# A two-block fp32 network on one core: the scheduler's cost estimates are replaced on three engines

## The chip, the core and the metric

The kernel runs on one core of a Trainium2 chip. A core has five engines that run side by side, each working through its own list of instructions in order: TensorE (PE in the profile; PEld is its loading of weights), VectorE (DVE), ScalarE (ACT), GpSimd (POOL) and SyncE (SP), which here issues the DMAs. Engines wait for each other through semaphores. The metric is the device time of one execution in microseconds (us); smaller is better.

## The reference, cut to what matters

Two blocks on 256 tokens of width 1024, all in fp32. The first block has a mixer (a short convolution, stick-breaking attention and retention, merged by gates), attention to a memory of 256 rows, and a squared-ReLU MLP of width 4096. The second block has a state-space mixer (SSD, 8 groups), a feed-forward net with a causal convolution (width 2816), a latent attention of 8 heads, and a second such feed-forward net; each is followed by a layer norm.

```python
h = rmsnorm(x, norm_mix_g); proj = h @ w_in            # 10 x 512 + 3 x 1024 columns
x = x + sum(sigmoid(gates) * up(conv, stick, ret)) @ w_o
x = x + memory_attention(rmsnorm(x), rmsnorm(mem), w_q, w_kv, w_out)
x = rmsnorm(x + square(relu(rmsnorm(x) @ w_up)) @ w_down)
h = layer_norm(ALPHA * x + ssd_mixer(x));  h = layer_norm(ALPHA * h + conv_ffn(h))
h = layer_norm(ALPHA * h + mla_attention(h)); h = layer_norm(ALPHA * h + conv_ffn(h))
```

## The kernel before, in words

**Weights.** All weight matrices lie in one array, cut into chunks of at most 128 partitions x 2048 floats (1 MB) in the order of their use. A chunk is loaded by a DMA into a raw tile (`wr`, two buffers) and split in two halves: ScalarE casts a half to the high part (`wh`, method `copy`), VectorE subtracts it from the raw half to get the low part (`wl`, method `sub`). Four split chunks are held at most (`HELD`). A product is three matmuls on TensorE (`mm3`): high x high, high x low, low x high. Activations are split the same way (`ah`, `al` and others), after transposes on TensorE into the `sm` banks of PSUM; the products go to the `mm` banks.

**Order of the work.** The program is written out at build time by a planner; on the chip every engine runs its list as it was written. The main line of the program walks through the matmuls stage by stage. After each group of matmuls it calls `tick`, which may insert, behind what has been issued so far, steps of background tasks (evacuations of PSUM, convolutions, softmax, norms, each a Python generator that yields where it would have to wait) and splits of weight halves. A step whose inputs come from TensorE, ScalarE or VectorE is inserted when the planner believes that they will be ready.

**What the planner believes.** `Plan` keeps one clock per engine (`t`). `enter` is called for each instruction: it starts at the later of the engine's clock and of the time when its operands are there (`after`, with a handover from engine to engine out of the table `LATE`, 0.05 to 0.22 us) and moves the clock by `cost`. `cost` has one formula for each engine. A matmul of 256 or more columns costs its columns at 2400 per us. On ScalarE an instruction costs its elements at 1200 per us and 0.05 us (from PSUM) or 0.093 us, and 0.093 us more for each further operand and for a sum. On VectorE it is elements at 960 per us and 0.068 us, and 0.06 us for each operand that is a column.

**Where the clocks are used.** `can_step` lets a task step if its inputs are ready by the clock of TensorE or of its own engine, and its engine is not over `AHEAD` (1.0 us) in front of TensorE; tasks marked `first` (norms) may be taken a little early (`EARLY`). `split_next` inserts a cast or a subtraction. It calls one late by a deadline: `need` is now plus the matmul time of the chunks that are split (`sums`, in units of `UNIT`) less the matmul time done (`work`), and 0.95 us are counted for a cast and 1.15 us for a subtraction. A split that is not late must leave room in front of a `first` task and must not be over `FILL` (0.8 us) ahead. At the end of a stage, the last chunks are kept and used for both halves of the tokens (`TAIL`), so that the norm of the first half runs beside the second half's matmuls; `skew` accounts for them.

The profile puts nearly every instruction on L284, the line of the helper that records them, so its groups are told apart by tiles.

Of the kernel before, what the change touches and what calls it, by code (L numbers as in the profile page):

```python
# [8 lines left out]
BF16 = mybir.dt.bfloat16  # L9
# [15 lines left out]
LATE = {("pe", "act"): 0.2, ("pe", "dve"): 0.2, ("act", "pe"): 0.22, ("dve", "pe"): 0.15, ("pool", "dve"): 0.06,  # L25
        ("pool", "act"): 0.06, ("pool", "pe"): 0.05, ("act", "pool"): 0.18, ("dve", "pool"): 0.16, ("act", "act"): 0.15,
        ("pe", "pe"): 0.0, ("dma", "act"): 0.95, ("dma", "dve"): 0.95, ("dma", "pe"): 0.95, ("dma", "pool"): 0.95}
UNIT = 6 / 2400
AHEAD = 1.0
FILL = 0.8  # L30
SOON = 0.0
# [258 lines left out]
class Plan:  # L290
# [62 lines left out]
    def cost(self, kind, name, out, ins, args, kw):  # L353
        n = 1
        for s, c in out.ap[1:]:
            n *= c
        psum = any(x.space == PSUM for x in ins)
        aps = sum(1 for x in ins[1:] if x.free_size() == 1)
        if kind == "pe":
            if name == "transpose":  # L360
                return 0.11
            if kw["rhs"].dtype == F32:
                m = kw["lhsT"].shape[-1]
                return 4 * max(n, m) / 2400 * (0.53 if m <= 64 else 1.0)
            return (n if n >= 256 or kw["rhs"].dtype == BF16 else 4 * n) / 2400
        if kind == "act":
            t = n / 1200 + (0.05 if psum else 0.093)
            if name in ("activation", "mul"):
                t += 0.093 * (len(ins) - 1) + (0.093 if "accum_out" in kw else 0)
            return t  # L370
        if kind == "dve":
            for x in ins[:1]:
                m = 1
                for s, c in x.ap[1:]:
                    m *= c
                n = max(n, m)
            if name == "reciprocal":
                return n / 160 + 0.07
            fast = name in ("tensor_copy", "tensor_scalar", "tensor_scalar_mul", "tensor_scalar_add") and not psum
            return n / (1920 if fast else 960) + 0.068 + (0.06 * aps if "scalar" in name else 0)  # L380
        if kind == "pool":
            return (0.3 + 0.16 * n if n < 3 else 0.6) if name == "tensor_tensor" else n / (280 if name == "tensor_copy" else 960) + 0.11
        return 0.0
# [88 lines left out]
class Kern:  # L472
    def __init__(self, nc, tc, a, dbg=None):
# [11 lines left out]
        self.work = self.skew = 0.0  # L485
        self.sums = np.concatenate([[0.0], np.cumsum([len(ks) * max(n, P) * UNIT for _, ks, _, n, _ in self.plan])])

# [197 lines left out]
    def mm3(self, outs, lhs, rhs, first, last, weights=True):  # L685
        passes = ((0, 0), (0, 1), (1, 0))
        if weights:
            self.work += sum(o.free_size() for o in outs) * 3 / 2400
        for q, (i, j) in enumerate(passes):
            for n, o in enumerate(outs):  # L690
                self.nc.tensor.matmul(o, lhsT=lhs[i], rhs=rhs[j][n] if isinstance(rhs[j], list) else rhs[j],
                                      start=first and q == 0, stop=last and q == 2, skip_group_check=True)
# [27 lines left out]
    def xstat(self, tag, nks, lhs, blocks, tail=0, after=None, before=None):  # L720
# [29 lines left out]
        if tail:  # L750
            chs = []
            for tau in range(2):
# [3 lines left out]
                for c in range(tail):  # L756
# [19 lines left out]
                    else:  # L776
                        self.skew = 0.0 if c == tail - 1 else self.skew + nk * chs[c][0].shape[2] * UNIT / 2
                    self.tick()
        return ps

    def wmixed(self, tag, act, nk, consumers, tasks=None):
# [4 lines left out]
        for tau in range(2):  # L786
            for c in range(n):
# [8 lines left out]
                if tau == 0:  # L796
                    self.skew = 0.0 if c == n - 1 else self.skew + nk * wh.shape[2] * UNIT / 2
                if tau:
# [637 lines left out]
    def ssd(self, h, act):  # L1436
# [259 lines left out]
        for tau in range(2):  # L1696
            got = [0]
            for i, (half, c) in enumerate(last):
                ch = so(half, c, (tau,), chs[i] if tau else None)
                chs.append(ch)  # L1700
                if tau == 0:
                    self.skew = 0.0 if i == 2 else self.skew + 2048 * UNIT / 2
                if i:
# [80 lines left out]
    def attention(self, h, act):  # L1784
# [106 lines left out]
        for tau in range(2):  # L1891
            for tag, nk, src, blocks in (("qr", 3, cq, [(0, 512)]), ("v", 2, ckv, [(0, 512), (512, D)])):
# [12 lines left out]
                else:  # L1905
                    self.skew = nk * wh.shape[2] * UNIT / 2 if tag == "qr" else 0.0
                if tag == "qr":
# [180 lines left out]
```

## Time and profile before

| | |
|---|---|
| median of 3 runs | 1233.27 us (1233.09 to 1234.08) |
| the profiled execution's own time | 1233.43 us |
| its span in the profile | 1231.7 us |
| TensorE busy | 1214.2 us, 99% of the span |
| weight loads busy | 1109.8 us, 90% |
| VectorE busy | 852.7 us, 69% |
| ScalarE busy | 718.0 us, 58% |
| DMA queue of the weights and inputs | 51.1% of 16 engines' time |

The profiled execution is one execution beside the timed ones. Its span runs from the first to the last instruction, and 1.73 us of its own time lie outside the span. Busy time is the union of the instructions' own intervals; where instructions of one engine overlap in the records, a mean duration is longer than the distance from one start to the next.

### The profile page before, as it was taken

The numbers are of one execution on the slowest core, as the hardware profiler recorded it, in microseconds if no ns is written. First come the engines' busy times: TensorE is split into PE (matmuls) and PEld (weight loads), VectorE is DVE, ScalarE is ACT, GpSimd is POOL, SyncE is SP. The second block draws the span as 40 slices with busy tenths as digits, with TensorE's granted clock in tenths as the row PEclk, the third lists the DMA queues.
The fourth block names the chain that finished last, engine by engine and source line by source line (L and its number), as shares of the span: only waits on it lengthen the run. The fifth ranks groups of instructions, "written<-read, shape, count | busy, mean of one in ns | idle before, by whom it ended". The sixth has DMA issues, their size and how long they took to land.

```text
span 1231.7 us, 20769 instructions
## 1 busy us (share of the span) xinstructions
PE 1214.2 (99%) x8468; PEld 1109.8 (90%) x8468; DVE 852.7 (69%) x1378; ACT 718.0 (58%) x1181; POOL 53.2 (4%) x85
## 2 busy tenths in 40 slices
PE   7999999999999999999999999999999999999997
PEld 5979999989989998888999898999988888999986
DVE  5666848677747765446887797888855866888853
ACT  5666546446536554345789765666643665666631
POOL 0011000000000000000111201000000000000000
PEclk9999999999999999999999999999999999999999
DMA  7643355546444556524556545555673442455560
GB/s 257 246 159 132 142 198 221 185 163 227 172 154 167 211 193 226 183 105 172 224 206 237 190 172 197 180 185 193 216 262 105 164 184 106 171 206 190 209 251 34
DMA packets 35425, 227.71 MB, mean 185 GB/s; under 512 B 4321, under 2 KB 4993, under 8 KB 11522
## 3 DMA queue, kind: packets, MB, share of 16 engines
q1 hardware_dynamic: 35330, 226.39, 51.1%
q8 instruction: 66, 1.08, 0.3%
q14 instruction: 29, 0.24, 0.1%
HBM read 225.27 MB, written 1.10 MB: 184 GB/s over the span
## 4 chain that ended last, share of the span: by engine, by line
PE 93%; DVE 3%; DMA 1%; ACT 1%; issue 0%; POOL 0%; SPq 0%; POOLq 0%; DVEq 0%; ACTq 0%
PE mm L284 84%; PE sm L284 9%; DMA wr<-wts 1%; DVE wl L284 1%; DVE x L284 1%; DVE tk L284 0%; POOL rs L284 0%; ACT wh L284 0%; SPq L284 0%; DVE dtw L284 0%; DVE ln L284 0%; DVE al L284 0%; ACT L284 0%; ACT tk L284 0%; POOLq L2084 0%
## 5 line engine op out<-in xcount | busy, mean ns | idle before, releaser
L284 DVE TENSOR_TENSOR wl<-wr,wh 128x1024 fp32r<-128x1024 f32 (+3 forms) x408 | 478.7, 1196 | 174.2 <-ACT wh L284 173.5
L284 ACT CAST wh<-wr 128x1024 fp32r<-128x1024 f32 (+3 forms) x408 | 403.9, 1030 | 160.4 <-PE mm L284 88.6
L284 PE MATMUL mm<-ah,wh 128*128 128x256 f32 (+1 forms) x1496 | 417.1, 279 | 0.0
L284 PE MATMUL mm<-ah,wl 128*128 128x256 f32 (+1 forms) x1496 | 413.6, 276 | 0.1
L284 PE MATMUL mm<-al,wh 128*128 128x256 f32 (+1 forms) x1496 | 413.4, 276 | 0.0
L284 PEld LDWEIGHTS mm<-ah,wh 128*128 128x128 f32 (+1 forms) x1496 | 280.2, 187 | 1.6 <-issue 1.1
L284 PEld LDWEIGHTS mm<-al,wh 128*128 128x128 f32 (+1 forms) x1496 | 280.3, 187 | 0.4
L284 PEld LDWEIGHTS mm<-ah,wl 128*128 128x128 f32 (+1 forms) x1496 | 280.2, 187 | 0.4 <-DVE wl L284 0.3
L284 DVE SCALAR_TENSOR_TENSOR r<-mm,pcol,r 128x255 f32<-128x255 f32 (+2 forms) x212 | 86.9, 474 | 35.1 <-ACT r L284 35.1
L284 PE MATMUL mm<-wl,ah 128*128 128x512 f32 (+3 forms) x320 | 106.1, 338 | 3.0 <-DVE wl L284 2.9
L284 PE MATMUL mm<-wh,ah 128*128 128x512 f32 (+3 forms) x320 | 108.7, 346 | 0.0
L284 PE MATMUL mm<-wh,al 128*128 128x512 f32 (+3 forms) x320 | 106.3, 338 | 0.5 <-DVE al L284 0.5
L284 PE MATMUL mm<-wh,gTh 128*128 128x512 f32 x304 | 96.2, 391 | 0.0
L284 PE MATMUL mm<-wl,gTh 128*128 128x512 f32 x304 | 95.6, 389 | 0.0
L284 PE MATMUL mm<-wh,gTl 128*128 128x512 f32 x304 | 95.5, 389 | 0.0
L284 ACT ACTIVATE r<-mm,pcol 128x256 f32<-128x256 f32 x96 | 48.9, 560 | 43.3 <-PE mm L284 43.3
L284 PEld LDWEIGHTS mm<-wl,ah 128*128 128x128 f32 x320 | 60.4, 190 | 10.0 <-DVE wl L284 4.6
L284 PEld LDWEIGHTS mm<-wh,gTl 128*128 128x128 f32 x304 | 57.1, 188 | 11.9
L284 PEld LDWEIGHTS mm<-wl,gTh 128*128 128x128 f32 x304 | 57.1, 188 | 11.8
L284 PEld LDWEIGHTS mm<-wh,gTh 128*128 128x128 f32 x304 | 56.7, 188 | 12.0 <-issue 0.6
L284 PEld LDWEIGHTS mm<-wh,al 128*128 128x128 f32 x320 | 60.2, 189 | 7.0 <-DVE al L284 1.2
L284 PEld LDWEIGHTS mm<-wh,ah 128*128 128x128 f32 x320 | 60.3, 189 | 6.5 <-issue 0.7
(296 smaller groups left out, 1576.6 us busy)
## 6 DMA issues: line engine op xcount, KB each, us to landing
wr<-wts SPq DMA_DIRECT2D x186, 1024.0 KB, 4.8
wr<-wts SPq DMA_DIRECT2D x11, 768.0 KB, 4.3
gb<-prow SPq DMA_DIRECT2D x12, 512.0 KB, 6.5
dec<-rows SPq DMA_DIRECT2D x8, 768.0 KB, 8.1
wr<-wts SPq DMA_DIRECT2D x4, 704.0 KB, 4.1
wr<-wts SPq DMA_DIRECT2D x4, 512.0 KB, 6.5
tk<-mem SPq DMA_DIRECT2D x2, 512.0 KB, 7.3
out<-x SPq DMA_DIRECT2D x4, 256.0 KB, 2.1
```

The lines of the kernel that those rows point to most:

```text
L284: r = f(*args, **kw)
```

## The change

The planner's estimates are changed. A matmul of 256 or more columns costs 17/16 of what it cost, and so do the unit of the deadline (`UNIT`) and the matmul time done (`work`). On ScalarE elements cost 1/1110 us in place of 1/1200, and the fixed part is 0.1 us for every source. On VectorE the fixed part is 0.11 us in place of 0.068. All other numbers of the planner, and all instructions that the program holds, stay; only the order in which they are written can differ (and, through the ScalarE clock, where a table is loaded in advance).

```diff
-UNIT = 6 / 2400
+UNIT = 6 * 17 / 16 / 2400
...
-            return (n if n >= 256 or kw["rhs"].dtype == BF16 else 4 * n) / 2400
+            return (n * 17 / 16 if n >= 256 else n if kw["rhs"].dtype == BF16 else 4 * n) / 2400
         if kind == "act":
-            t = n / 1200 + (0.05 if psum else 0.093)
+            t = n / 1110 + 0.1
...
-            return n / (1920 if fast else 960) + 0.068 + (0.06 * aps if "scalar" in name else 0)
+            return n / (1920 if fast else 960) + 0.11 + (0.06 * aps if "scalar" in name else 0)
...
         if weights:
-            self.work += sum(o.free_size() for o in outs) * 3 / 2400
+            self.work += sum(o.free_size() for o in outs) * 3 * 17 / 16 / 2400
```

## Rows read from the trace of the kernel before

**Rows 1.** The page's first part: busy us (share of the span) xinstructions of each engine.

```profile
PE 1214.2 (99%) x8468; PEld 1109.8 (90%) x8468; DVE 852.7 (69%) x1378; ACT 718.0 (58%) x1181; POOL 53.2 (4%) x85
```

**Rows 2.** Windows: stretch, its length, busy us (xinstructions) per engine, clock, DMA.

```profile
0.00:20.00 20.00, 13.48 (x42) 8.61 (x43) 10.75 (x24) 10.39 (x17) 1.57 (x7) 1.00 0.83 288
300.00:395.00 95.00, 94.94 (x631) 86.52 (x630) 60.84 (x85) 51.00 (x82) 1.10 (x2) 1.00 0.47 171
395.00:550.00 155.00, 155.00 (x989) 140.20 (x988) 87.29 (x92) 72.60 (x89) 0.55 (x1) 1.00 0.52 188
550.00:566.00 16.00, 15.55 (x84) 12.72 (x83) 9.12 (x15) 5.67 (x11) 0.55 (x1) 1.00 0.35 133
566.00:580.00 14.00, 13.87 (x119) 13.27 (x117) 8.38 (x20) 10.64 (x17) 0.00 (x0) 1.00 0.42 152
745.00:763.00 18.00, 17.84 (x86) 14.53 (x85) 11.45 (x21) 9.71 (x17) 1.63 (x2) 1.00 0.67 245
937.00:964.00 27.00, 25.62 (x140) 22.09 (x139) 20.39 (x45) 13.89 (x30) 2.68 (x3) 1.00 0.39 134
964.00:1030.00 66.00, 65.91 (x403) 56.25 (x403) 45.19 (x108) 41.05 (x93) 0.70 (x1) 1.00 0.46 168
1030.00:1062.00 32.00, 31.27 (x228) 28.76 (x227) 24.65 (x40) 20.31 (x33) 1.87 (x2) 1.00 0.37 132
1223.00:1231.70 8.70, 0.71 (x4) 0.25 (x2) 4.11 (x11) 2.02 (x6) 0.93 (x1) 0.83 0.17 61
```

**Rows 3.** Timeline of TensorE: start us, us, instruction; 36 and 16 matmuls lie between starts.

```profile
400.02 0.28 PE L284 MATMUL mm<-ah,wl 128*128 128x256 f32 x1
...
404.10 0.28 PE L284 MATMUL mm<-ah,wl 128*128 128x256 f32 x1
...
500.45 0.62 PE L284 MATMUL mm<-wh,gTh 128*128 128x512 f32 x2
...
504.07 0.62 PE L284 MATMUL mm<-wh,gTl 128*128 128x512 f32 x2
```

**Rows 4.** Groups by form: xcount, busy us, mean ns of one, idle before and releasers.

```profile
L284 DVE TENSOR_TENSOR wl<-wr,wh 128x1024 fp32r<-128x1024 f32 x376 | 451.0, 1222 | 157.8 <-ACT wh L284 157.1
...
L284 ACT CAST wh<-wr 128x1024 fp32r<-128x1024 f32 x376 | 380.0, 1050 | 154.3 <-PE mm L284 86.3 <-DMA wr<-wts 63.7 <-issue 2.6
...
L284 PE MATMUL sm<-cst,tk 128*128 128x128 f32 x116 | 17.9, 283 | 2.4 <-DVE tk L284 2.2 <-ACT tk L284 0.2
```

**Rows 5.** Timelines of VectorE and of ScalarE, us 1045 to 1061 (runs of equal instructions merged).

```profile
1045.72 2.35 DVE L284 TENSOR_TENSOR wl<-wr,wh 128x1024 fp32r<-128x1024 f32 x2
1047.99 1.28 DVE L284 TENSOR_TENSOR al<-sm,ah 128x512 fp32r<-128x512 f32 x2
...
1057.58 1.64 DVE L284 SCALAR_TENSOR_TENSOR r<-sm,pcol,r 128x255 f32<-128x255 f32 x4
1059.14 2.35 DVE L284 TENSOR_TENSOR wl<-wr,wh 128x1024 fp32r<-128x1024 f32 x2
...
1057.49 2.01 ACT L284 CAST wh<-wr 128x1024 fp32r<-128x1024 f32 x2
1059.39 1.04 ACT L284 ACTIVATE r<-sm,pcol 128x256 f32<-128x256 f32 x2
1060.30 0.60 ACT L284 COPY tk<-mm 128x512 f32<-128x512 f32 x1
```

**Rows 6.** Chain that ended last, around us 949 and 1040: start us, us, what.

```profile
949.07 0.81 DVE wl L284
...
1040.02 1.14 DVE wl L284
```

**Rows 7.** TensorE's waits over the span: us in total, times, longest us.

```profile
PE sm L284 <- DVE x L284: 0.7, 3, 0.3
```

**Rows 8.** Timeline of TensorE, us 942 to 944: two matmul pairs, the first behind four transposes.

```profile
942.14 0.70 PE L284 MATMUL mm<-wh,gTh 128*128 128x512 f32 x2
...
943.15 0.62 PE L284 MATMUL mm<-wh,gTl 128*128 128x512 f32 x2
```

## The prediction

> **What bounds the kernel now.** I read the page's busy times first, then cut the span into windows at the joints between stages, then looked inside the windows at the single engines' timelines. The first view says that TensorE is busy for 1214.2 of 1231.7 us [rows 1]; 17.5 us are idle. The windows say where [rows 2]: 6.52 us in the first 20 us (the first weights and inputs are still arriving, with the DMA engines 83% busy), 7.99 us in the last 8.7 us (the last layer norm, behind the last matmul), and 0.06 + 0.45 + 0.13 + 0.16 + 1.38 + 0.09 + 0.73 = 3.00 us in seven windows between. All these windows are joints: a norm ends one stage and begins the next, and TensorE meets transposes or a low weight half that are not there yet. Everywhere else TensorE is fed without a gap; 395 to 550 us is such a stretch, 989 matmuls and no idle time.
>
> So the kernel is bound by the list of its matmuls. Nothing in the diff removes an instruction; it can only reorder the lists of the three engines. What it can win is idle time of TensorE at the joints, and a little where transposes are put between matmuls.
>
> A page of the Trainium skill speaks against reading it so: "Perfetto Trace Analysis", section "Identifying the Most-Contended Engine", calls matmul busy time a bad measure of what is left and takes the busy share of the weight loads instead. By that share, 90% [rows 1], an estimate of headroom would be 10% of the span, 122 us. The row of 395 to 550 us decides against it here: the loads are busy for 140.20 of 155.00 us [rows 2] while the 512-column matmuls inside it follow each other at their steady distance [rows 3]; the loads wait for matmuls, not the other way round.
>
> **What the change does to the estimates.** First the true numbers, as distances from start to start in full queues:
> - A 256-column matmul: 36 starts in 404.10 - 400.02 = 4.08 us, 113.3 ns; a 512-column one: 16 in 3.62 us, 226.3 ns [rows 3]. The old estimate is 256/2400 = 106.7 ns and 213.3 ns, 6% short; the new one 113.3 and 226.7 ns, right.
> - The subtraction of a weight half on VectorE: two in 1047.99 - 1045.72 = 2.27 us, 1.135 us each [rows 5]. Old 1024/960 + 0.068 = 1.135, right; new 1.177, 3.7% long.
> - A convolution step on VectorE (255 elements, PSUM, a column operand): four in 1.56 us, 0.390 [rows 5]. Old 0.394, right; new 0.436, 12% long.
> - The cast of a weight half on ScalarE: two in 1059.39 - 1057.49 = 1.90 us, 0.950 [rows 5]. Old 0.946, right; new 1024/1110 + 0.1 = 1.023, 7.6% long.
> - An activation of 256 elements from PSUM with scale and bias: two in 0.91 us, 0.455 [rows 5]. Old 0.213 + 0.05 + 0.186 = 0.449, right; new 0.517, 14% long.
>
> The durations of single instructions are longer: 1222 ns for the subtraction, 1050 ns for the cast [rows 4]. The new formulas move towards those. But consecutive instructions overlap by 0.09 to 0.10 us (1.222 - 1.135, 1.050 - 0.950), and the planner adds its costs one behind the other, while the handover to another engine stands in a table of its own that isn't touched. So on TensorE an estimate that was short becomes right, and on the other two, ones that were right become long.
>
> What decides an order is the ratio between engines. Before, VectorE and ScalarE looked 113.3/106.7 = 1.062 times as slow against TensorE as they are. After, VectorE looks 1.04 (subtractions, 451.0 of its 852.7 us [rows 1, 4]) to 1.12 times as slow, by shares about 0.53 x 1.037 + 0.47 x 1.10 = 1.07; ScalarE 1.076 (casts, 380.0 of 718.0 us) to 1.14, about 0.53 x 1.076 + 0.47 x 1.12 = 1.10. Taken together the change is very nearly one of the unit of time: all three clocks run 4 to 15% longer, and their ratios move by +1% and +3.5%. Only what keeps its size (handovers, the limits of 1.0 and 0.8 us, the 1.15 and 0.95 us of the deadline, transposes, DMA times) gets 6% smaller beside the rest. So I expect close decisions to tip here and there, with no drift.
>
> **The terms of the sum**, against the profiled execution's own 1233.43 us (0.16 us above the median of the runs):
> - The stretches with no idle time: 0. Cover: TensorE's own list of matmuls, full; a step that is moved there moves within the idle time of VectorE or ScalarE (67.7 and 82.4 us of 155.0 between 395 and 550 us [rows 2]).
> - Start and end: 0. The start waits for weights, the end is a chain with no weights left to order. From both sides: nothing to win without data; to lose, one subtraction in front of the second norm, 1.1 us [rows 5], which I take for unlikely.
> - The joints: from -3.00 us (all idle time closed [rows 2]) to +4.5 us (below). The deadline test: `need` grows by 1/16 of the split matmul time in stock (a 1 MB chunk is 48 matmuls of 113.3 ns, 5.4 us, so 0.3 us for each), against 0.04 or 0.08 us more for each split; splits count as late a little less often, so a subtraction may give way to a norm at 949 and 1040 us, where it now stands on the chain for 0.81 and 1.14 us [rows 6]. But behind the norm the same subtractions must still run before the next stage's matmuls, so most of that comes back. The waits of transposes for the norm, 0.7 us in all [rows 7], should shrink, as norm steps are now given more time. I take -0.5.
> - Insertions of transposes: the matmul pair behind four transposes takes 0.70 instead of 0.62 us [rows 8], so an insertion costs about 0.08 us beside its own work. One group alone has 116 transposes, 29 insertions by fours [rows 4]. If a dozen more or fewer stand alone, that is 1.0 us either way; I take 0.
> - Table loads and DMAs: the DMAs are issued in the same order from a subtraction's end; I take 0.
>
> Sum: 1233.43 - 0.5 = 1232.9; I say 1233.0.
>
> **The rivals.**
> - *The joints close.* With TensorE's own speed right, transposes and norm steps are put where their inputs are there, and the idle time goes: 1233.43 - 3.00 - 0.5 (a few insertions merged) = 1229.9. For it: the gaps are where short chains of 512-element steps meet TensorE. Against: the largest one, 1.38 us between 937 and 964 us, lies where VectorE is busy for 20.39 of 27.00 us [rows 2] with the few split buffers full; order alone hardly helps. 0.23.
> - *Subtractions land on the norms' chains* (the other sign). With ScalarE thought 7.6% slower at casts, a cast and its subtraction come one place later, and at the four joints with the thickest chains (windows at 550, 745, 937 and 1030 us) the subtraction falls between the steps of the norm, which TensorE waits for: 4 x 1.135 = 4.5 us, 1237.9. It decides from three joints of the four. For it: it happens already at two places [rows 6]. Against: the lateness test loosens. 0.21.
> - *TensorE's estimate is now too long*, so that the others seem fast and transposes are put in too early. If two thirds of the step of 6% were too much, 4%, a norm of up to 7.99 us, as at the end [rows 2], would come 0.3 us later than planned; if two in three of 29 insertions [rows 4] met that, it would be 5.8 us, 1239.2. The starts of 113.3 and 226.3 ns speak against it [rows 3]. The Trainium skill, "TensorE: Matmul & The Clock Gate", section "Back-to-back issue gap", would have it so: columns / 2.4 GHz + 2.5 ns, 109.2 and 215.8 ns. The trace does not agree: its excess is 6.6 and 13 ns and grows with the columns. 0.04.
> - *Nothing tips* or the tips cancel, which is also the case that the change doesn't do what it says, since it brings durations into a model that wants distances: 1233.4, part of the forecast.
>
> **How the numbers follow.** About 0.2% (2.5 us) is what a measurement of this kernel can tell from no change. The forecast (1233.0, own range 1231.0 to 1235.5) has 0.52, all of it within that bound; the joints that close 0.23, faster; the two slower rivals 0.25. So faster 0.23, same 0.52, slower 0.25. For 8 in 10 the range goes from 1229.6 (under the closed joints) to 1238.2 (just over the subtractions at all four).
>
> **What the profile after would show.** Right: TensorE with 2 to 4.5 us idle between 20 and 1223 us, the same count of instructions but perhaps a table load or two, starts 113 and 226 ns apart in the full stretches. The joint at 937 to 964 us keeps about 1 us. The first rival is right if the seven windows fall to under 0.6 us together; the second if a subtraction stands between two norm steps at three or four joints and the idle time there is over 5 us. I am wrong altogether if idle time appears inside a full stretch (the state-space stage has the busiest VectorE and ScalarE), where a tipped order would starve TensorE of split weights.

## The result and the profile after

The changed kernel takes 1259.32 us (median of 4 runs, 1258.19 to 1263.83) against 1233.32 us for the kernel before in the same comparison: ratio 1.0214 (95% interval 1.0202 to 1.0226), slower by 26 us. The forecast was 1233.0 us with a range from 1229.6 to 1238.2.

The page's first part, of the changed kernel (answers to [rows 1]; span 1256.8 us):

```profile
PE 1221.9 (97%) x8468; PEld 1113.5 (89%) x8468; DVE 854.0 (68%) x1378; ACT 719.1 (57%) x1178; POOL 49.6 (4%) x85
```

The lists hold the same work: 8468 matmuls, 1378 VectorE instructions, and three ScalarE instructions fewer (the planner loads a table in advance, by a dummy activation, four times instead of seven; the 24 table loads stay). The span grew by 25.1 us, of which TensorE's busy time is 1221.9 - 1214.2 = 7.7 us and its idle time 34.9 - 17.5 = 17.4 us. Both need a cause. The windows say where (columns as in [rows 2]: length, busy us of each engine, TensorE's granted clock, DMA share and GB/s):

```profile
0.00:20.00 20.00, 14.05 (x45) 8.91 (x46) 11.15 (x24) 10.44 (x18) 1.57 (x7) 1.00 0.83 294
370.00:398.00 28.00, 26.52 (x208) 25.07 (x207) 19.29 (x23) 16.12 (x24) 1.40 (x1) 1.00 0.41 151
398.00:550.00 152.00, 152.00 (x973) 137.56 (x972) 84.58 (x89) 71.84 (x88) 0.15 (x1) 1.00 0.54 192
550.00:572.00 22.00, 20.51 (x115) 17.00 (x114) 12.94 (x19) 9.05 (x16) 0.95 (x2) 1.00 0.40 145
572.00:675.00 103.00, 103.00 (x777) 94.81 (x776) 81.64 (x138) 89.63 (x172) 16.61 (x20) 1.00 0.59 215
675.00:690.00 15.00, 11.41 (x74) 10.07 (x73) 14.12 (x24) 13.00 (x21) 0.00 (x0) 0.89 0.57 198
762.00:798.00 36.00, 33.36 (x233) 30.32 (x232) 25.31 (x41) 19.82 (x34) 2.00 (x2) 1.00 0.40 152
955.00:990.00 35.00, 29.83 (x165) 25.91 (x164) 24.07 (x58) 15.81 (x35) 2.39 (x3) 1.00 0.39 135
1045.00:1080.00 35.00, 29.49 (x179) 26.84 (x179) 22.00 (x35) 16.52 (x28) 1.87 (x2) 0.90 0.42 151
1248.00:1256.80 8.80, 0.43 (x2) 0.01 (x1) 4.02 (x9) 1.92 (x6) 0.93 (x1) 0.72 0.16 61
```

Length less TensorE's busy time is its idle time: 5.95 us at the start and 8.37 at the end, nearly as before (6.52 and 7.99), and 1.48 + 1.49 + 3.59 + 2.64 + 5.17 + 5.51 = 19.88 us in six places between, where the kernel before has 3.00 us in all [rows 2]. Five are joints that it has too. One, at 675 to 690 us, ends the state-space stage, where the kernel before has no idle time. The long stretches between the joints (398 to 550, 572 to 675) stay full.

What TensorE waits for, in total over the span (us, times, longest):

```profile
PE mm L284 <- DVE wl L284: 11.8, 10, 3.2
PE sm L284 <- ACT r L284: 3.5, 1, 3.5
PE sm L284 <- ACT tk L284: 3.5, 3, 1.6
```

The first line is matmuls that wait for a weight half's low part; in the kernel before it is 2.9 us. The second is one wait, the new one at the end of the state-space stage. The third, 0.2 us before, is transposes that wait for a copy of their input on ScalarE. The norm, which the prediction watched, is not the main loser (transposes wait for its `x` for 0.6 us, against 0.7 [rows 7]); the weights are late.

**One joint followed (370 to 398 us).** Up to 372 us the two traces agree to some hundredths of a us. Then VectorE takes the residual additions `x` before the subtraction `wl`, which in the kernel before came first. Timelines of VectorE (dots stand for lines between), first the kernel before, then the changed one:

```profile
372.44 1.22 DVE L284 TENSOR_TENSOR wl<-wr,wh 128x1024 fp32r<-128x1024 f32 x1
...
374.77 1.22 DVE L284 TENSOR_TENSOR wl<-wr,wh 128x1024 fp32r<-128x1024 f32 x1
```

```profile
372.61 0.69 DVE L284 SCALAR_TENSOR_TENSOR x<-mm,x 128x512 f32<-128x512 f32 x1
...
375.77 1.22 DVE L284 TENSOR_TENSOR wl<-wr,wh 128x1024 fp32r<-128x1024 f32 x1
...
378.76 3.48 DVE L284 TENSOR_TENSOR wl<-wr,wh 128x1024 fp32r<-128x1024 f32 x3
```

The two halves of a chunk share one raw buffer, so the second half's subtraction (374.77 us before; changed, the first of the three at 378.76) is its last reader. There are two raw buffers (`RAW = 2`), and the DMA that refills one stands behind that subtraction. SyncE's queue, before and then changed:

```profile
376.01 14.42 SPq L284 DMA_DIRECT2D wr<-wts  x4
```

```profile
380.04 11.62 SPq L284 DMA_DIRECT2D wr<-wts  x4
```

The second half's subtraction starts 3.99 us later, the DMA 4.03. The chain that ended last, of the changed kernel, carries that on (start us, us, what):

```profile
380.04 4.78 DMA wr<-wts
...
384.90 1.05 ACT wh L284
...
385.98 2.37 DVE wl L284 x2
...
388.37 4.83 DMA wr<-wts
...
393.28 1.05 ACT wh L284
394.33 0.49 ACT t L284
394.82 0.94 ACT wh L284
395.76 0.53 ACT gTh L284
396.29 0.48 ACT tk L284
...
396.82 0.66 PE sm L284 x4
```

DMA, cast, subtraction, DMA, and then late casts stand between the steps of the next stage's gate, for which TensorE's transposes at 396.82 us wait. The first subtraction was moved by 3.3 us. Of the 1.48 us of idle time, 0.63 came at once (377 to 379 us, waits for the low part and for the norm), and 0.85 came 20 us later, at 396.82 us.

**The new stall (state-space stage).** The chain of the changed kernel at 678 to 687 us:

```profile
678.13 2.27 DVE wl L284 x2
...
680.66 0.80 DVE yTl L284 x2
...
681.49 1.98 ACT wh L284 x2
683.47 0.63 ACT yTh L284 x2
684.10 0.64 ACT r L284
...
684.78 1.99 PE sm L284 x8
```

Two casts (1.98 us) and two evacuations (0.63) stand ahead of the last gate activation on ScalarE, and TensorE waits 3.5 us. VectorE and ScalarE are busy for 14.12 and 13.00 of these 15 us, so little can be put off there without cost; that is an argument, as no run moves a step of this stretch alone.

**The busy time.** The granted clock explains most of the 7.7 us. Windows of 2 us behind the stall:

```profile
684.00:686.00 2.00, 1.22 (x6) 1.13 (x7) 2.00 (x3) 2.00 (x5) 0.00 (x0) 0.82 0.24 98
686.00:688.00 2.00, 2.00 (x7) 1.62 (x7) 2.00 (x4) 2.00 (x3) 0.00 (x0) 0.50 0.46 78
688.00:690.00 2.00, 2.00 (x11) 1.59 (x10) 2.00 (x3) 0.03 (x1) 0.00 (x0) 0.83 0.84 352
```

0.50 is 1.2 of 2.4 GHz. The three windows lack 0.18 + 0.50 + 0.17 = 0.85 of 2 us, up to 1.7 us of work. Of the 123 windows of 10 us from 20 to 1250 us, three are below 1.00: 680 to 690, 1060 to 1070 and 1070 to 1080 us, each at 0.83, together 3 x 1.7 = 5.1 us at most, since these windows count the clock of idle time too; the kernel before has none from 20 to 1220 us. The other 2.6 us are not resolved (0.57 of them is in the first 20 us; the transposes stand between the matmuls in 81 runs, against 82 before, so it is not more insertions).

### The profile page after: what moved, and what is told of

Read it like the earlier page. It is cut to its first block, busy times and chain, and to the rows that moved or that the text cites. A ratio compares the mean times of both kernels' runs of the same rounds, so it can differ in the third digit from the quotient of the medians.

```text
span 1256.8 us, 20781 instructions
## 1 busy us (share of the span) xinstructions
PE 1221.9 (97%) x8468; PEld 1113.5 (89%) x8468; DVE 854.0 (68%) x1378; ACT 719.1 (57%) x1178; POOL 49.6 (4%) x85
## 4 chain that ended last, share of the span: by engine, by line
PE 88%; DVE 5%; DMA 3%; ACT 2%; issue 1%; POOL 1%; SPq 0%; POOLq 0%; DVEq 0%; ACTq 0%
PE mm L284 79%; PE sm L284 9%; DMA wr<-wts 2%; DVE wl L284 2%; ACT wh L284 1%; DVE x L284 1%; POOL rs L284 1%; DVE r L284 0%; DVE tk L284 0%; ACT tk L284 0%; DVE al L284 0%; DMA cst<-cst 0%; ACT r L284 0%; ACT ah L284 0%; DVE ln L284 0%
## 5 line engine op out<-in xcount | busy, mean ns | idle before, releaser
L284 PEld LDWEIGHTS mm<-wh,gTh 128*128 128x128 f32 x304 | 56.7, 188 | 12.6 <-ACT r L284 0.9
L284 PEld LDWEIGHTS mm<-wh,gTl 128*128 128x128 f32 x304 | 57.1, 188 | 11.9
```

The costliest lines, as they stand in the source:

```text
L284: r = f(*args, **kw)
```

## The experiments

The letters in the expectations are theories. A: the planner's fixed limits, `FILL` = 0.8 us above all, keep their size while the clocks they are compared with run faster. B: the matmul estimate that was 6% short was a margin that kept weights early. C: the kernel before sits in a hollow, and a shift of either sign loses. D: an order flip is dear because a put-off subtraction holds its raw buffer and delays the next DMA. E, the prediction's own view: a flip costs at most a subtraction's length and is hidden. D': the deadline, which counts a chunk's casts and subtractions but not the DMA behind them, puts splits off too long. F: no order has room for both, the norm's steps and the splits.

**The parts alone.** `pe_only` takes the three TensorE terms of the diff, `dve_only` the one VectorE term, `no_dve` all but that; `fill_09` is the whole change with a wider limit. (In the tables, the ratio is to the kernel before in the same comparison, and the clock is TensorE's mean granted clock in the profiled execution.)

```
dve_only:  before,  + 0.068  ->  + 0.11
fill_09:   changed, FILL = 0.8  ->  FILL = 0.9
```

> Only TensorE's part of the change (matmul cost, unit of the deadline, work done times 17/16); ScalarE and VectorE keep the old estimates. Theory A (a subtraction at a joint misses the limit FILL of 0.8 us because VectorE's clock now stands further ahead; its raw buffer comes free later, the next weights land later, TensorE starves): 1229 to 1238 us. Rival B (the old, short matmul estimate was a hidden margin in the deadline; taking it away makes every split late): 1248 us or more.

> Only VectorE's part (0.11 in place of 0.068). Theory A: 1243 us or more, with idle TensorE at the joints. Rival B: 1230 to 1237 us, since TensorE's estimate is the old one.

> The whole change less VectorE's part. Theory A: 1243 us or less. Rival B: 1250 us or more, as TensorE's part is in it.

> The whole change, and the limit FILL at 0.9 us in place of 0.8, so that a subtraction is let in with VectorE's clock up to 0.9 us ahead. Theory A: 1245 us or less, and the joint at 370 to 398 us idle for less than 0.3 us (1.5 us with the change alone). Rival B: 1253 us or more, the limit is not what makes splits late.

| kernel | median us | ratio (95%) | clock |
|---|---|---|---|
| pe_only | 1245.98 | 1.0099 (1.0071 to 1.0128) | 0.998 |
| dve_only | 1256.10 | 1.0181 (1.0166 to 1.0196) | 0.991 |
| no_dve | 1249.37 | 1.0125 (1.0110 to 1.0141) | 0.995 |
| fill_09 | 1246.75 | 1.0104 (1.0087 to 1.0120) | 0.995 |

Every part loses, and the parts don't add: 12.2 us for TensorE's terms and 22.3 for VectorE's against 26.0 for all. VectorE's 42 ns nearly suffice alone, so most of the loss comes without B. But only `dve_only` came out as a theory said (A). `pe_only` (four runs from 1241.97 to 1250.52 us), `no_dve` and `fill_09` fell between A's and B's forecasts, and the 12.2 us for TensorE's terms fit neither. ScalarE's terms were not tried alone. Widening `FILL` by 0.1 us returns 12.6 us, and the joint at 370 us is full again:

```profile
370.00:398.00 28.00, 28.00 (x216) 26.66 (x214) 20.18 (x25) 16.97 (x25) 1.10 (x2) 1.00 0.43 151
675.00:690.00 15.00, 11.41 (x76) 10.38 (x75) 13.96 (x26) 13.96 (x23) 0.00 (x0) 0.80 0.50 175
```

The limit decides at that joint. It doesn't at 675 to 690 us, where 3.59 us idle stay.

**Small shifts, and all limits scaled.** Three kernels move one estimate of the kernel before; the fourth scales `AHEAD`, `FILL`, `EARLY` and the constants of the deadline and room tests of the changed kernel by 17/16, as the estimates were.

```
dve_plus4:        before, + 0.068  ->  + 0.072
dve_minus42:      before, + 0.068  ->  + 0.026
pe_half_percent:  before, the three TensorE terms * 201 / 200
```

> The kernel before with VectorE's fixed part at 0.072 in place of 0.068, a tenth of the change's step, 4 ns an instruction. Theory C (the limits were tuned on exactly the old estimates, and the decisions are so near to ties that a shift of any size or sign tips several of them, each for some us): 1238 us or more. Theory A (longer estimates make VectorE's clock pass the limit; a tenth of the shift tips little): 1231 to 1236 us.

> The kernel before with VectorE's fixed part at 0.026, the change's step with the other sign. Theory C: 1240 us or more, as with the step upward (1256.1). Theory A: 1231 to 1237 us, since a clock that stands behind passes no limit.

> The kernel before with TensorE's three terms times 201/200 in place of 17/16. Theory C: 1238 us or more. Theory A and rival B (a margin of 6% was taken away): 1231 to 1236 us, since half a per cent is a twelfth of the step.

> The whole change with the limits of can_step and split_next (FILL, AHEAD, EARLY, the counts of the deadline, the room in front of a norm) times 17/16 as well. Theory A (the limits kept their size while the clocks got longer): 1232 to 1243 us. Theory C (it is another point, as good as any that is not tuned): 1243 to 1258 us.

| kernel | median us | ratio (95%) | clock |
|---|---|---|---|
| dve_plus4 | 1242.25 | 1.0072 (1.0057 to 1.0087) | 0.995 |
| dve_minus42 | 1240.06 | 1.0051 (1.0036 to 1.0066) | 0.998 |
| pe_half_percent | 1239.73 | 1.0051 (1.0036 to 1.0066) | 0.995 |
| limits_scaled | 1259.16 | 1.0200 (1.0183 to 1.0217) | 0.993 |

Four ns on VectorE's estimate cost 8.5 us, 42 ns the other way 6.3, half a per cent on TensorE's 6.0. Every shift loses, as C says; a loss with either sign is shown for VectorE's estimate, TensorE's was only raised. B's forecast (up to 1236 us) is missed as well: a twelfth of the step costs half of what the step costs. A falls in its general form: with the limits scaled the time is that of the changed kernel (1.2 us above C's range). C had expected that several decisions tip, each for some us. The two smallest shifts lose in one stage: the joint at 370 us stays full, and the state-space stage stalls (570 to 710 us in the kernel before, in `pe_half_percent` and in `dve_plus4`):

```profile
570.00:710.00 140.00, 139.87 (x1022) 127.22 (x1021) 113.07 (x185) 115.49 (x216) 22.81 (x22) 1.00 0.56 204
```

```profile
570.00:710.00 140.00, 136.37 (x965) 122.65 (x964) 110.59 (x181) 113.04 (x214) 15.95 (x22) 0.98 0.54 196
```

```profile
570.00:710.00 140.00, 134.39 (x949) 120.59 (x949) 113.19 (x183) 113.43 (x212) 20.28 (x22) 0.98 0.55 199
```

The idle time there is 3.63 and 5.61 us in place of 0.13, and the clock takes up to 3.4 us more in each (0.81 and 0.85 in `pe_half_percent`, 0.76 and 0.90 in `dve_plus4`, from 680 to 690 and from 690 to 700 us); the idle time between the start and the end outside this stretch is 3.01 and 2.76 us in place of 2.85. So the two losses lie there. It is not the same wait: in `pe_half_percent` matmuls wait for a low part on VectorE, in `dve_plus4`, as in the changed kernel, transposes wait for an activation `r` on ScalarE. The line of `pe_half_percent`:

```profile
PE mm L284 <- DVE yTl L284: 3.5, 1, 3.5
```

`dve_minus42` differs: 1.55 us idle in this stretch and 5.9 outside.

**One decision.** At the joint at 370 us one subtraction is put off by hand in the kernel before (`tip_one`) or let in by hand in the changed kernel (`untip_one`), by a limit that is 0.1 us narrower or wider for the two halves of that one weight chunk. D is also tried with a third raw buffer, in both kernels.

```
tip_one:    before,  t["dve"] <= now + FILL - (0.1 if self.n_prep == 61 else 0)
untip_one:  changed, t["dve"] <= now + FILL + (0.1 if self.n_prep == 61 else 0)
raw3_*:     RAW, HELD = 2, 4  ->  RAW, HELD = 3, 4
```

> The kernel before with one decision tipped: at the joint of 370 to 398 us (chunk 61) the limit for a subtraction is 0.7 in place of 0.8 us, so that the first half's subtraction comes behind the second norm's first steps, as in the changed kernel. Theory D (the price of a tip is the raw buffer: it comes free later, the next weights land later and TensorE waits for them): 1.2 to 1.8 us of idle TensorE at that joint (0.1 before) and 1235 us or more. Rival E (a tipped subtraction costs its own 1.1 us at most and is hidden): under 0.4 us idle there, 1232 to 1235 us in all.

> The changed kernel with the same decision tipped back (0.9 us for chunk 61 alone). Theory D: idle TensorE between 370 and 398 us under 0.4 us (1.48 with the change), and the total lower by 1.5 to 5 us, 1254 to 1258 us. Rival E: the joint stays at 1.2 us or more.

> The changed kernel with three raw buffers in place of two (RAW), so that a DMA needn't wait for the last subtraction. Theory D: 1245 us or less, the weights no longer land late at the joints. Rival E: 1253 us or more.

> The kernel before with three raw buffers. Theory D: 1228 to 1237 us, since nothing lands late there. Theory C (its limits are tuned on exactly its state, and any other order costs): 1238 us or more, although the buffer can only take waits away.

| kernel | median us | ratio (95%) | clock |
|---|---|---|---|
| tip_one | 1235.96 | 1.0019 (1.0010 to 1.0028) | 0.999 |
| untip_one | 1257.60 | 1.0190 (1.0174 to 1.0205) | 0.993 |
| raw3_changed | 1251.79 | 1.0148 (1.0131 to 1.0165) | 0.997 |
| raw3_before | 1243.74 | 1.0079 (1.0064 to 1.0094) | 0.996 |

The joint's window in the kernel before, in `tip_one` and in `untip_one`:

```profile
370.00:398.00 28.00, 28.00 (x229) 27.32 (x228) 20.07 (x25) 17.76 (x27) 0.55 (x1) 1.00 0.44 154
```

```profile
370.00:398.00 28.00, 26.42 (x208) 25.00 (x208) 19.92 (x25) 16.96 (x26) 1.39 (x1) 1.00 0.42 156
```

```profile
370.00:398.00 28.00, 28.00 (x223) 26.98 (x221) 19.89 (x25) 17.03 (x27) 0.55 (x1) 1.00 0.43 154
```

One flip makes the changed kernel's joint inside the kernel before (28.00 - 26.42 = 1.58 us idle, and 1235.96 - 1233.98 = 1.98 us of time), and undoing it in the changed kernel fills the joint and returns 1.7 us (the intervals of the two ratios touch, so that time alone isn't clear of the noise). So for this joint the flip is shown in both directions as the cause of the idle time, and E is refuted: a flip costs more than the 1.135 us of the subtraction, and nothing hides it. At this joint D can be read off too. With the third buffer the subtractions stand as late behind the additions as in the changed kernel, and the joint is idle for 0.63 us (`raw3_changed`):

```profile
370.00:398.00 28.00, 27.37 (x209) 25.73 (x208) 19.59 (x25) 17.50 (x26) 1.40 (x1) 1.00 0.39 151
```

The part that came at once stays; the 0.85 us that came by the late DMA is gone. In all, the third buffer takes 7.5 us off the changed kernel, where D had said 14 or more, so D holds in part; and it costs the kernel before 9.8 us, against D's forecast (1237 us at most) and in line with C's.

**The deadline.** It is tested 2 or 4 us earlier, so that splits count as late sooner:

```
deadline2: 1.15 * (subs + copies) + 1.0 > need        ->  ... + 3.0 > need
           ... 1.15 * (subs + copies - 1)) + 2.2 > need  ->  ... + 4.2 > need
deadline4: 5.0 and 6.2
```

> The changed kernel with the deadline 2 us earlier (3.0 and 4.2 in place of 1.0 and 2.2). Theory D' (splits are put off until the deadline, which doesn't count the DMA behind them): 1240 to 1252 us and the joint at 1045 to 1080 us idle for less than 2.5 us (5.5 with the change). Rival F (VectorE and ScalarE have no room there in any order): 1255 us or more.

> The same with 4 us. Theory D': at most the time of 2 us plus 3 us. Rival F: 1257 us or more.

> The kernel before with the deadline 2 us earlier. Theory C (limits tuned on exactly this state): 1238 us or more, a loss where the changed kernel has a gain. Theory D' alone: 1230 to 1236 us.

> The changed kernel with the deadline 2 us earlier and three raw buffers. Theory D': both lift the same wait, so no more than 4 us better than the better of the two alone (1251.8 with three buffers). Rival F: 1251 us or more.

| kernel | median us | ratio (95%) | clock |
|---|---|---|---|
| deadline2_changed | 1248.24 | 1.0118 (1.0103 to 1.0133) | 0.996 |
| deadline4_changed | 1255.55 | 1.0176 (1.0159 to 1.0193) | 0.990 |
| deadline2_before | 1245.63 | 1.0100 (1.0085 to 1.0115) | 0.996 |
| deadline2_raw3_changed | 1256.34 | 1.0184 (1.0168 to 1.0199) | 0.995 |

Two us return 11.1 us, and the changed kernel's worst joint falls from 5.51 us idle to 2.45 (`deadline2_changed`):

```profile
1045.00:1080.00 35.00, 32.55 (x249) 30.60 (x248) 26.50 (x44) 22.06 (x37) 1.87 (x2) 1.00 0.41 148
```

The clock of that window is back at 1.00. So the deadline did put splits off too long at that joint (D'). But four us lose most of it, more than D' allows, two cost the kernel before 11.9 us, and with a third buffer beside them the gain goes as well (1256.34 us, where F had said 1251 or more): helps that work alone don't add either. The windows show where they lose: between 570 and 710 us TensorE is idle for 4.50 us in `deadline2_changed`, 14.14 in `deadline4_changed` and 9.76 in `deadline2_raw3_changed`, against 4.63 in the changed kernel, so what the joints gain the state-space stage takes. F falls by the kernel before itself, whose order has room for both (0.73 us idle at that joint [rows 2]). No kernel of the sixteen reaches the kernel before.

## Why the prediction was wrong

**What failed: "close decisions tip here and there, with no drift".** The prediction took tips as noise around zero. All eight kernels that move one thing in the kernel before lose: 12.2 (`pe_only`), 22.3, 8.5, 6.3, 6.0, 2.0, 9.8 and 11.9 us. A full list of matmuls has little to win from a flip, as the prediction itself had found (3.00 us at the joints), and a flip can make TensorE idle for longer than that. With so little to win, tips could hardly cancel.

**What failed: the price of a tip.** The sum had -0.5 us for the joints, and at most +4.5; measured, five joints have 1.48 + 1.49 + 2.64 + 5.17 + 5.51 = 16.29 us idle, where the kernel before has 3.00 in all. The upper bound came from four subtractions of 1.135 us in front of the norm. For a subtraction put off behind the norm a gain was counted, cut down because "the same subtractions must still run before the next stage's matmuls, so most of that comes back". More than that came back: the price of a put-off subtraction was taken as its own length at most, without what stands behind it. That "the DMAs are issued in the same order from a subtraction's end; I take 0" was true of the order and missed the time: the end moved, and the DMA with it, 4.0 us at 376 to 380 us. With two raw buffers there is no stock behind it; with three, the part of the wait that came by the DMA was gone. Measured: 1.58 us idle for a single flip, and 5.17 and 5.51 us at the joints at 955 and 1045 us, against 1.38 and 0.73 before [rows 2]. At the last one TensorE waited 3.16 and 2.12 us for two subtractions. The chain shows the first of them behind the norm (start us, us, what):

```profile
1061.18 1.41 DVE x L284 x2
1062.59 1.15 DVE wl L284
...
1063.78 0.52 PE mm L284 x2
```

The prediction had named this flip, that a subtraction "may give way to a norm at 949 and 1040 us", and counted it as a small gain. Its second rival had the right sign and named four of the six places, but with subtractions in front of norm steps; in the trace the norm is in front, and the matmuls wait.

**What failed: full stretches at 0.** The cover named, VectorE's and ScalarE's idle time, was read from 395 to 550 us. At the state-space stage's end it isn't there (14.12 and 13.00 of 15 us are busy), and 3.59 us are lost. The long full stretches did stay full. This stage was the easiest to upset: a shift of 4 ns cost 8.5 us, and the idle time and the clock of that stage account for it. The text had named this stage under "wrong altogether if", without a chance or a price.

**What was missing: the clock.** The sum had no term for it. Some of the longer waits cost a second time, as slow matmuls, up to 5.1 us in all.

**What held:** the lists are the same but for three ScalarE instructions; start and end move by -0.57 and +0.38 us of idle time; the insertions, taken as 0, are as many as before; the third rival (TensorE's estimate too long) isn't needed, since VectorE's part alone loses nearly all, and the estimate isn't too long: 113.3 ns was read from the matmuls `mm<-ah,wl` [rows 3], and the last section shows 118 ns for `mm<-wh,ah`.

**What stays open.** The flips behind the stalls in the state-space stage were not isolated. A stall comes there with 4 or 42 ns more on VectorE's estimate and with half a per cent on TensorE's, not always at the same wait, and not with `tip_one`. `untip_one` and `fill_09` don't lift it (4.44 and 4.66 us idle from 570 to 710 us). The places at 550 and 762 us were not tried by themselves. The shares of the single flips in the 26 us are therefore not known beyond the windows above.

## What to carry to other kernels

Where the bounding engine is 99% busy and an order is made by a planner, this case says to price a change of its numbers as a loss with a size to be measured: try the smallest change of either sign first (here 4 ns), before reasoning on whether the numbers became truer. Follow a put-off step to the buffer that it frees and the DMA behind that, since part of the bill comes a transfer and a split later, at another place. Look first at the stage where the side engines have the least room. A wait of some us can cost a second time by the clock.

## What the runs showed of the hardware

After some waits TensorE didn't run at full clock. It had been idle for 3.16 us at 1063.78 us and for 2.12 at 1070.07, and the same matmuls then ran slowly for a while (timeline of TensorE, changed kernel):

```profile
1070.29 0.28 PE L284 MATMUL mm<-wh,al 128*128 128x256 f32 x1
...
1070.76 0.28 PE L284 MATMUL mm<-wh,ah 128*128 128x256 f32 x1
...
1071.22 0.42 PE L284 MATMUL mm<-wh,ah 128*128 128x256 f32 x1
...
1073.99 0.41 PE L284 MATMUL mm<-wl,ah 128*128 128x256 f32 x1
...
1074.53 0.28 PE L284 MATMUL mm<-wl,ah 128*128 128x256 f32 x1
...
1076.30 0.28 PE L284 MATMUL mm<-wl,ah 128*128 128x256 f32 x1
```

From 1071.22 us thirteen steps from start to start take 2.77 us, 213 ns each; from 1074.53 us fifteen take 1.77 us, 118 ns each. The slow ones begin about 1 us behind the end of the wait: the engine was at full clock when it resumed at 1070.07 us (four steps in 0.47 us, 118 ns each) and fell at 1071 us. The wait of 2.45 us at 966.87 us was followed by a stretch at 1.00. The Trainium skill, "TensorE: Matmul & The Clock Gate", section "What's actually happening", says that the array's clock is halved when the engine has been idle; the granted clock of 0.50 at 686 to 688 us agrees, and the fall here came when the work had already begun again.
